# Cached token keys turned in squares by Vector with queries spread by token group, and memory queries' single rows copied first

## The chip, the cores and the metric

The kernel runs on one core of a Trainium2 chip. The time is the device time of one execution in microseconds, from the first instruction to the last; the median of several runs is compared. The engines are PE (matrix products and transposes into PSUM), DVE (Vector), ACT (Scalar), POOL (GpSimd) and SP, which issues most DMAs. Each engine works through its own list of instructions in order and waits where an instruction needs another engine's result.

## The reference

One layer of a decoder, run on a prompt of 512 rows and on 8 samples of 4 new rows each (32 rows), with the same weights. The layer is an mLSTM head group and a differential-attention head group side by side, one output projection, a cross-attention into 256 memory tokens, and a gated feed-forward part with a short convolution. The change touches the two attentions of the samples. The differential attention of a sample has 4 heads with two components of 64 dimensions, 256 cached tokens and its own 4 new ones:

```python
def diff_attend(q, k, v, mask, lam):
    s = jnp.einsum('bqhcd,bkhcd->bhcqk', q.astype(jnp.float32), k.astype(jnp.float32)) * (DA_QK_DIM ** -0.5)
    s = jnp.where(mask[None, None, None], s, -jnp.inf)
    p = jax.nn.softmax(s, axis=-1)
    a = p[:, :, 0] - lam * p[:, :, 1]
    return jnp.einsum('bhqk,bkhd->bqhd', a, v.astype(jnp.float32))
```

For the samples k and v are the cached rows followed by the new ones, and new row t sees all cached tokens and the new ones up to t. The memory attention has 4 heads of 256 dimensions, 256 tokens that differ from sample to sample, and a plain softmax. The mLSTM part also writes out the samples' updated states, C = decay * C + k v^T for 8 samples and 4 heads.

## The kernel before, in words

The program goes through the layer stage by stage: input projection (L485), mLSTM and differential attention with their DMAs, output projection (L411 to L413), memory attention, feed-forward. A scheduler puts the instructions that the code emits into one fixed list for each engine, by its own estimate of when each can start; two helpers bind it: `burst(t)` keeps an instruction right behind t, and `tc.issue_after(t)` keeps it somewhere behind t. `pipe(n, stages...)` emits the stages of n items a step apart, and `F.run` puts filler work between (here the gating of the mLSTM output, L1039 to L1046). Tiles come from pools with a fixed number of buffers: six staging tiles (`stage()`, printed as wst), four weight slots (tag W), three PSUM buffers of tag at, five of tag mm.

**The state update of the samples.** For each of 8 pairs of a sample group and a head, POOL makes vz (L942), PE multiplies it with the keys kS (L1006, tile mlus, a buffer of tag at), and DVE does four updates (L1008), 32 in all. The old and new states lie in staging tiles. The input projection's last part (L485 with hT and wslot) runs on PE at the same time.

**The prompt's differential attention.** For each of 16 pairs of a query block and a head: scores on PE (L1256, L1257, tile sda), maximum on DVE (L1259), exponential on ACT (L1260), normalising on DVE (L1262 to L1264, result pda), transposes on PE (L1272, tile tpa), copy on ACT (L1274), product with the values on PE (L1284, tile oda). The number of keys grows from 128 to 512. PE takes the turn of one pair between the scores of later ones.

**The samples' differential attention, cached keys.** It runs a step at a time beside the prompt's. `dk_load` fetches two pages of 128 tokens by 4 heads by 128 into a staging tile. `dk_turn` makes 8 transposes of 128x128 on PE (L1228) and copies each page's four from PSUM to kT, one page by ACT, one by DVE (L1229); POOL appends the 4 new keys' columns (L1224). `dk_scores` works on two samples at once: 4 products each of 32x260 (L1241), each to its own 32 rows of the result, which hold 4 heads by 2 components by 4 samples by 4 rows, of which one sample's are wanted. DVE adds the mask of the new tokens (L1244), and takes the maximum (L1052); ACT takes the exponential with its sum (L1053). When all 8 are done, `sample_softmax` builds selecting matrices from 1/sum and lambda, and 8 products (L1072) normalise, subtract and put the samples below each other; then two transposes on PE (L1085) and eight copies on ACT (L1089) give daz, from which the products with the values follow (L1340), and for the new tokens L1318, L1320 and L1345.

**The memory attention.** The queries' projection gives 8 groups of 128 columns (`ev_q(m)`). From its PSUM result ACT makes qh (L1429), DVE ql = result - qh (L1430), and ACT qs, the samples' 32 rows (L1432). After every second group `mq_spread` copies qs to the diagonal blocks of qx, by POOL, the last group half by ACT (L1415, L1418). The cached keys of the memory are turned by DVE in place in 32x32 squares (L1502), and the scores are products of them with qx (L1519), for a token group and a head at a time; e picks one half of the heads. The components' sums (L1535), one softmax with maxima and sums over the token groups (L1539 to L1544, L1552 to L1556), and products with an identity that turn the result (L1565) follow. Beside it the prompt's memory scores (L1450, tile sca), exponentials (L1456, tile cp), normalising (L1459), transposes (L1468, tile cpt) go on.

## Time and profile before

| what | value |
|---|---|
| median of 3 runs | 942.89 us (941.97 to 945.42) |
| the profiled execution, its own time | 941.59 us |
| its span in the trace | 939.8 us |
| PE busy | 914.5 us, 97% of the span |
| DVE, ACT, POOL busy | 608.5, 378.2, 221.6 us |
| mean granted clock of PE | 0.994 |
| stretch of the samples' cached keys on PE | 245.4 us (first L1228) to 272.9 (last L1241 starts) |
| first product of the output projection (L411) | 299.95 us |
| first memory score product (L1519) | 432.9 us |

A row of the order of time gives the start in us, the length of the group in us, engine, line, operation, output and inputs, shape, and the number of instructions; in square brackets the idle time before it and what ended it. A product in full precision shows as two records on PE. A busy PE counts overlapping matmuls once. The span starts with the first instruction; the execution's own time is some 1.8 us longer.

### The profile page before, as it was taken

How to read it: one execution, taken by the hardware profiler on the slowest of the kernel's cores; microseconds unless marked ns; L12 is line 12 of the kernel's file. 1: busy time of each engine (PE TensorE's matmuls, PEld its weight loads, DVE VectorE, ACT ScalarE, POOL GpSimd, SP SyncE). 2: the span in 40 equal slices, each digit the busy share in tenths (PEclk: the TensorE clock that was granted, in tenths of full speed). 3: DMA queues.
4: the chain of work that ended last, by engine and by line, in shares of the span. 5: the costliest groups of instructions: out<-in, count | busy, mean ns of one | idle time of the engine just before them, and what ended most of it. 6: DMA issues, size and time to landing. Idle time of an engine off the chain costs nothing. (4 is left out here: it accounts for less than half of the span.)

```text
span 939.8 us, 17453 instructions
## 1 busy us (share of the span) xinstructions
PE 914.5 (97%) x6778; PEld 799.9 (85%) x6778; DVE 608.5 (65%) x1130; ACT 378.2 (40%) x728; POOL 221.6 (24%) x474
## 2 busy tenths in 40 slices
PE   7999999999999999998999999999999999999995
PEld 5899787879866778997877899889988998999974
DVE  5845144565887439586744778637757785676767
ACT  5745233344576447624534533322212222222232
POOL 6611000024442116471000553001100110110114
PEclk9999999999999999999999999999999999999998
DMA  8950023335780439957845642062054204412023
GB/s 274 317 187 8 1 90 138 90 107 157 247 292 7 141 112 314 311 183 238 343 155 159 198 130 72 27 179 69 8 153 121 88 21 109 139 48 90 24 94 117
DMA packets 120834, 130.59 MB, mean 139 GB/s; under 512 B 8599, under 2 KB 86264, under 8 KB 120752
## 3 DMA queue, kind: packets, MB, share of 16 engines
q1 hardware_dynamic: 114568, 125.96, 42.9%
q10 hardware_dynamic: 6184, 3.53, 1.2%
q8 instruction: 53, 0.87, 0.4%
q14 instruction: 29, 0.24, 0.1%
HBM read 112.54 MB, written 16.93 MB: 138 GB/s over the span
## 5 line engine op out<-in xcount | busy, mean ns | idle before, releaser
L485 PE MATMUL mm<-fT,wslot 128*128 128x256 f32 x1872 | 236.0, 288 | 0.0
L485 PEld LDWEIGHTS mm<-fT,wslot 128*128 128x128 f32 x1872 | 234.4, 188 | 1.8 <-issue 0.8
L146 ACT CAST wslot<-wst 128x1024 fp32r<-128x1024 f32 x125 | 130.7, 1049 | 255.5 <-issue 70.8
L147 DVE TENSOR_TENSOR wslot<-wst,wslot 128x1024 fp32r<-128x1024 f32 x125 | 154.7, 1241 | 78.3 <-ACT wslot L146 77.8
L1836 PE MATMUL mm<-wslot,act 128*128 128x512 f32 (+1 forms) x180 | 69.3, 387 | 0.0
L1839 PE MATMUL mm<-wslot,act 128*128 128x512 f32 (+1 forms) x172 | 67.0, 391 | 0.0
L1840 PE MATMUL mm<-wslot,act 128*128 128x512 f32 (+1 forms) x172 | 66.8, 392 | 0.0
L1738 POOL COPY cvo<-u 128x2 f32<-128x2 f32 x43 | 10.4, 242 | 217.2 <-DVE u L1736 217.2
L411 PE MATMUL mm<-wslot,hT 128*128 128x512 f32 x128 | 51.3, 402 | 0.0
L413 PE MATMUL mm<-wslot,hT 128*128 128x512 f32 x128 | 51.0, 400 | 0.0
L485 PE MATMUL mm<-hT,wslot 128*128 128x256 f32 (+1 forms) x384 | 50.9, 289 | 0.0
L412 PE MATMUL mm<-wslot,hT 128*128 128x512 f32 x128 | 50.8, 397 | 0.0
L1733 DVE TENSOR_TENSOR u<-mm,rsb 128x256 f32<-128x256 f32 x43 | 18.1, 423 | 48.8 <-PE mm L485 48.8
L485 PEld LDWEIGHTS mm<-hT,wslot 128*128 128x128 f32 x384 | 49.2, 188 | 0.5 <-issue 0.2
L1836 PEld LDWEIGHTS mm<-wslot,act 128*128 128x128 f32 x180 | 34.3, 191 | 8.0 <-issue 0.8
L1840 PEld LDWEIGHTS mm<-wslot,act 128*128 128x128 f32 x172 | 32.3, 188 | 6.9 <-issue 0.4
L1839 PEld LDWEIGHTS mm<-wslot,act 128*128 128x128 f32 x172 | 32.3, 188 | 6.9
L1750 ACT ACTIVATE c<-c 128x560 f32<-128x560 f32 x21 | 14.1, 672 | 56.8 <-DVE c L1744 56.7
L1744 DVE SCALAR_TENSOR_TENSOR c<-u,cvT,c 128x560 f32<-128x560 f32 x43 | 34.3, 798 | 0.9
L1743 DVE SCALAR_TENSOR_TENSOR c<-u,cvT,c 128x560 f32<-128x560 f32 x43 | 34.1, 793 | 0.2
L1851 DVE TENSOR_TENSOR yp<-mm,yp 128x512 f32<-128x512 f32 (+1 forms) x41 | 27.1, 672 | 4.8 <-PE mm L1840 4.6
L413 PEld LDWEIGHTS mm<-wslot,hT 128*128 128x128 f32 x128 | 24.1, 188 | 5.0
(493 smaller groups left out, 1858.3 us busy)
## 6 DMA issues: line engine op xcount, KB each, us to landing
wst<-in_w_up_dram SPq DMA_DIRECT2D x42, 512.0 KB
wst<-in_w_in_dram SPq DMA_DIRECT2D x28, 512.0 KB
wst<-in_w_down_dram SPq DMA_DIRECT2D x20, 512.0 KB
kvt<-in_cache_mem_k_dram SPq DMA_DIRECT2D x10, 512.0 KB
kvt<-in_cache_mem_v_dram SPq DMA_DIRECT2D x10, 512.0 KB
wst<-in_w_mk_dram SPq DMA_DIRECT2D x8, 512.0 KB
xb<-in_x_prompt_dram SPq DMA_DIRECT2D x8, 512.0 KB
wst<-in_cache_dk_dram SPq DMA_DIRECT2D x16, 256.0 KB
```

The source lines that it names most:

```text
L146: nc.scalar.copy(out=hi, in_=src)
L147: (eng or nc.vector).tensor_tensor(out=lo, in0=src, in1=f32(hi), op=SUB)
L411: mm(ps[b], lhsT=xt.hi(k, c0, c0 + n), rhs=s[:, 0, kk, :], start=(k == 0), stop=False)
L412: mm(ps[b], lhsT=xt.hi(k, c0, c0 + n), rhs=s[:, 1, kk, :], start=False, stop=False)
L413: return mm(ps[b], lhsT=xt.lo(k, c0, c0 + n), rhs=s[:, 0, kk, :], start=False, stop=(k == nk - 1))
L485: mm(ps[i], lhsT=s[:, l, k, :], rhs=x(k, c0, c1), start=(k == 0 and j == 0), stop=(k == 7 and j == 2))
L1743: STT(out=c, in0=u[:, 1:EXT - 1], scalar=w[1], in1=c, op0=MUL, op1=ADD)
L1744: STT(out=c, in0=u[:, 0:EXT - 2], scalar=w[0], in1=c, op0=MUL, op1=ADD)
L1836: mm(ps, lhsT=t[:, 0, c0:c0 + P], rhs=s[:, 0, i % 2, cs], start=st, stop=False)
L1839: mm(ps, lhsT=t[:, 0, c0:c0 + P], rhs=s[:, 1, i % 2, cs], start=False, stop=False)
L1840: return mm(ps, lhsT=t[:, 1, c0:c0 + P], rhs=s[:, 0, i % 2, cs], start=False, stop=en)
L1851: VTT(out=y, in0=ps, in1=y, op=ADD)
```

## The change

Part one. The samples' cached keys are no longer transposed on PE: `dk_turn` is now one DVE instruction that turns the staging tile of 128x1024 in place in squares of 32x32 (L1235). The queries are spread beforehand into qx, a tile in a weight slot, cleared (L1214) and filled by 16 copies (L1217) on POOL, so that each token group of 32 rows meets its own queries; 8 products of 32x128 per sample (L1262), in bursts of their own for each sample, give the scores of all token groups, and ACT copies them to sc (L1265). The staging tile is held until these products. The scores of the new tokens come from `dk_new` (L1241, L1248 to L1251). When all samples are done, `dk_sum` adds the parts with 32 products (L1280), and one softmax for all samples (`da_softmax`, L1087 to L1102) takes maxima and sums over the token groups with two small 32-column transposes each (`over_groups`, L1055 to L1060); `attend` turns the result with 32 products (L1073) and two copies (L1076). The kT tiles, the per-sample mask, maximum and exponential, and L1072, L1085 and L1089 go. `over_groups`, `hcols` and `attend` are now shared with the memory part, whose own text moves up unchanged.

Part two. In `ev_q` the samples' rows qs and the spread are emitted ahead of qh and ql (L1464 to L1469), and `mk_scores` goes over e outside and over the samples inside, with both samples' PSUM tiles open at once (L1542 on).

```diff
+    def over_groups(t, n, u, w, op):
+        nc.vector.transpose(out=u, in_=t)
+        VRED(out=v2(w, TS), in_=u.rearrange("p (n g t) -> p n t g", n=2, g=4), axis=AX.X, op=op)
+        if op == ADD:
+            nc.vector.reciprocal(out=w, in_=w)
+        VCP(out=u.rearrange("p (n g t) -> p n g t", n=2, g=4), in_=v2(w, TS).unsqueeze(2).broadcast_to([P, 2, 4, TS]))
+        nc.vector.transpose(out=t, in_=u)
...
+        for c in range(2):
+            for h in range(H):
+                for g in range(4):
+                    with burst(t):
+                        t = mm(pT[NS * g:NS * g + NS, c * P + NS * h:c * P + NS * h + NS], lhsT=a[:, 64 * h + NS * c:64 * h + NS * c + NS],
+                               rhs=view(ident, 4 * g, [(16, NB), (1, TS)]), start=True, stop=True).ins
...
+    qx = wp.tile([P, 4, NB, H, 4, TS], F32, name="qx", tag="W")
+    nc.gpsimd.memset(qx, 0.0)
+    for g in range(4):
+        for j in range(4):
+            nc.gpsimd.tensor_copy(out=qx[NS * g:NS * g + NS, j, :, :, g, :],
+                                  in_=dqT[NS * j:NS * j + NS, :, SEQ:].rearrange("p h (b t) -> p b h t", t=TS))
...
     def dk_turn(b):
-        kt = kts[b] = wp.tile([P, H, 260], F32, name="kT", tag="W")
-        nc.gpsimd.tensor_copy(out=kt[:, :, 256:260], in_=dkT[:, :, SEQ + TS * b:SEQ + TS * (b + 1)])
-        for g in range(2):
-            ps = at("tpk")
+        nc.vector.transpose(out=kst[b], in_=kst[b])
...
-                tr(ps[:, h * P:(h + 1) * P], kst[b][g][:, h * P:(h + 1) * P], ident)
-            (VCP if g else nc.scalar.copy)(out=kt[:, :, g * P:(g + 1) * P], in_=v2(ps, P))
...
     def dk_scores(b):
-        if b % 2 == 0:
-            return
...
+        for e in range(2):
+            for j in range(4):
+                with burst(t):
+                    t = mm(ps[NS * j:NS * j + NS, e * P:e * P + P].rearrange("p (h c t) -> p h c t", h=2, c=2),
+                           lhsT=qx[:, j, b, 2 * e:2 * e + 2].rearrange("p h g t -> p (h g t)"),
+                           rhs=view(kst[b], 256 * e + NS * j, [(P, 2), (512, 2), (1, NS)]), start=True, stop=True).ins
+        nc.scalar.copy(out=sc[:, b], in_=ps)
...
             if i == 1:
                 nc.scalar.mul(out=qs[:, m, :], in_=ps[:, n:n + NS], mul=1.0 / 16.0)
                 if m % 2 == 1:
                     mq_spread(m // 2)
+            nc.scalar.mul(out=q, in_=ps[:, :n], mul=1.0 / 16.0)
+            STT(out=ql[m // 4][:, m % 4, c0:c0 + n], in0=ps[:, :n], scalar=1.0 / 16.0, in1=f32(q), op0=MUL, op1=SUB)
```

What this does to the order of PE, where the input projection ends. Before (mm is the projection, mlus the state update's products, sda and tpa the prompt's scores and turns, tpk the turns of the samples' keys):

```order
L485 MATMUL mm<-hT_263,wslot 128x288
L1006 MATMUL mlus<-vz,kS 128x512 x2
L1256 MATMUL sda<-dkT,dqT 128x128
L1257 LDWEIGHTS cb
L1257 MATMUL sda<-cb 128x128
L1256 MATMUL sda<-dkT,dqz 128x128
L1257 LDWEIGHTS cb
L1257 MATMUL sda<-cb 128x128
L1256 MATMUL sda<-dkT,dqT 128x128
L1228 MATMUL tpk<-cpk,wst 128x128 x4
L1257 LDWEIGHTS cb
L1257 MATMUL sda<-cb 128x128
```

Six of the eight L1006 stand further ahead, 8 to 11 projection products apart, the first 65 products before the projection's end. After, behind the projection's end (sx is the new tokens' scores, ssc the samples' scores, mlt the gating's transposes):

```order
L1006 MATMUL mlus<-vz,kS 128x512
L1292 MATMUL sda<-dkT,dqz 128x128
L1293 LDWEIGHTS cb
L1293 MATMUL sda<-cb 128x128
L1006 MATMUL mlus<-vz,kS 128x512 x3
L1248 MATMUL sx<-dkT,qw 128x32 x2
L1262 MATMUL ssc<-wst,qx 32x128 x8
L1006 MATMUL mlus<-vz,kS 128x512
L1248 MATMUL sx<-dkT,qw 128x32 x4
L1039 MATMUL mlt<-cpk,mlh 128x128 x4
L1248 MATMUL sx<-dkT,qw 128x32 x2
L1039 MATMUL mlt<-cpk,mlh 128x128 x8
L1308 MATMUL tpa<-cpk,pda 128x128
```

The first two L1006 stand 13 and 5 products before the projection's end and the third behind the first prompt scores; the last four rows of that kind are here, behind the projection and mixed with the first samples' scores. The turns tpk are gone, and the first tpa comes behind the gating's transposes.

DVE, in the same place. Before, from the first state update to the first pda (kT is a copy of the turned keys):

```order
L1008 SCALAR_TENSOR_TENSOR wst<-wst,dec,mlus 128x128 x20
L1022 TENSOR_TENSOR gq<-gq,mlrs 128x1
L1008 SCALAR_TENSOR_TENSOR wst<-wst,dec,mlus 128x128 x4
L1024 TENSOR_SCALAR mlhs<-numS,gq 128x128
L1008 SCALAR_TENSOR_TENSOR wst<-wst,dec,mlus 128x128 x8
L1259 TENSOR_REDUCE nm<-sda 128x1 x4
L1229 COPY kT<-tpk 128x4x128
L1262 RECIPROCAL rc<-su 128x2
L1229 COPY kT<-tpk 128x4x128
L1263 TENSOR_SCALAR rc<-rc,su,nlam 128x1
L1262 RECIPROCAL rc<-su 128x2
L1264 SCALAR_TENSOR_TENSOR pda<-pda,rc 128x128
```

After, from the first state update on:

```order
L1008 SCALAR_TENSOR_TENSOR wst<-wst,dec,mlus 128x128 x8
L1295 TENSOR_REDUCE nm<-sda 128x1
L1008 SCALAR_TENSOR_TENSOR wst<-wst,dec,mlus 128x128 x4
L1295 TENSOR_REDUCE nm<-sda 128x1 x2
L1008 SCALAR_TENSOR_TENSOR wst<-wst,dec,mlus 128x128 x4
L1295 TENSOR_REDUCE nm<-sda 128x1
L1008 SCALAR_TENSOR_TENSOR wst<-wst,dec,mlus 128x128 x8
L1298 RECIPROCAL rc<-su 128x2
L1008 SCALAR_TENSOR_TENSOR wst<-wst,dec,mlus 128x128 x4
L1298 RECIPROCAL rc<-su 128x2
L1235 STREAM_TRANSPOSE wst<-wst 128x1024
L1299 TENSOR_SCALAR rc<-rc,su,nlam 128x1 x2
```

The updates are now mixed with the prompt's maxima and the first of six transposes of the keys (wst) that stand here; two others stand further ahead. The third pda, for which the third tpa waits, stood before at the end of this run of work:

```order
L1259 TENSOR_REDUCE nm<-sda 128x1 x2
L1244 TENSOR_TENSOR ssc<-ssc,cpk 128x4 x2
L1052 TENSOR_REDUCE snm<-ssc 128x1 x2
L1045 TENSOR_TENSOR mltm<-mlt,soT 128x512
L1262 RECIPROCAL rc<-su 128x2
L1045 TENSOR_TENSOR mltm<-mlt,soT 128x512 x2
L1263 TENSOR_SCALAR rc<-rc,su,nlam 128x1
L1259 TENSOR_REDUCE nm<-sda 128x1 x2
L1045 TENSOR_TENSOR mltm<-mlt,soT 128x128
L1264 SCALAR_TENSOR_TENSOR pda<-pda,rc 128x128
```

And after:

```order
L1045 TENSOR_TENSOR mltm<-mlt,soT 128x128
L1235 STREAM_TRANSPOSE wst<-wst 128x1024
L1295 TENSOR_REDUCE nm<-sda 128x1 x2
L1298 RECIPROCAL rc<-su 128x2
L296 COPY xts<-mltm 128x128
L1235 STREAM_TRANSPOSE wst<-wst 128x1024
L1299 TENSOR_SCALAR rc<-rc,su,nlam 128x1
L1298 RECIPROCAL rc<-su 128x2
L1300 SCALAR_TENSOR_TENSOR pda<-pda,rc 128x128
```

All eight transposes of the keys are now ahead of the third pda; before, its row followed the copies, masks and maxima of the first samples.

ACT, in the memory attention where the last two groups of queries are taken. Before:

```order
L1456 ACTIVATE cp,csu<-sca,cnm 128x256 x2
L1429 ACTIVATE qh<-mm 128x256 x2
L146 CAST pT<-cpt 128x256
L1432 ACTIVATE qs<-mm 128x32
L1415 COPY qx<-qs 32x2x8x4 x8
```

And after:

```order
L1491 ACTIVATE cp,csu<-sca,cnm 128x256 x2
L1468 ACTIVATE qh<-mm 128x256
L1465 ACTIVATE qs<-mm 128x32
L1468 ACTIVATE qh<-mm 128x256
L146 CAST pT<-cpt 128x256
L1450 COPY qx<-qs 32x2x8x4 x8
```

The samples' rows qs now stand ahead of the last qh, and the spread (x8) behind the same cast of pT as before. PE at the first scores of the memory's keys, before:

```order
L1450 MATMUL sca<-mkT,qh 128x256 x2
L1450 MATMUL sca<-mkT,ql 128x256
L1519 MATMUL ssc<-wst,qx 32x2x32 x64
L1468 MATMUL cpt<-cpk,cp 128x128 x4
L1450 MATMUL sca<-mkT,qh 128x256 x2
```

And after:

```order
L1485 MATMUL sca<-mkT,ql 128x256
L1554 MATMUL ssc<-wst,qx 32x2x32 x34
L1503 MATMUL cpt<-cpk,cp 128x128 x4
L1554 MATMUL ssc<-wst,qx 32x2x32 x30
L1485 MATMUL sca<-mkT,qh 128x256 x2
```

The 64 products are now in two pieces with the four transposes of cp between them; the first 32 of them are those of the first half of the heads for both samples.

More of the change, by code (lines that the diff above doesn't have):

```diff
@@ new lines, in dk_scores, with dk_sum @@
+        nc.scalar.copy(out=sc[:, b], in_=ps)
+        last[0] = t
+    last = [None]
+    def dk_sum():
+        t = None
+        for i in range(NB // 2):
+            for c in range(2):
+                r = slice(64 * c, 64 * c + 64)
+                for h in range(2):
+                    for e in range(2):
+                        o = 48 * h + 16 * (1 - e)
+                        with tc.issue_after(last[0]) if t is None else burst(t):
+                            t = mm(hcols(pS[c][NS * i:NS * i + NS], h), lhsT=con("selE")[r, o:o + NS],
+                                   rhs=hcols(sc[r, 2 * i + e], h), start=(e == 0), stop=(e == 1)).ins
@@ L1290, in da_end @@
             da_post(outs[i // H], P, i // H * P)
[L1292 to L1293 removed]
     W.nslots = 0
     prompt = pipe(4 * H, da_soft, lambda i: None, da_turn, da_av, da_end)
[L1298 to L1299 removed]
+    sc = S([P, NB, 256], F32, "sc")
+    gs = T2([P, 136], "gs")
+    nc.gpsimd.memset(gs, 1.0)
+    xn = gs[:, 128:136]
     for t, _ in enumerate(pipe(NB, dk_load, dk_turn, dk_scores)):
```

170 lines of the change are left out of this document (70 added, 100 removed).

## Prediction

> **What bounds the kernel now.** I read the page first, then the waits of the PE, then busy time by stretch, then the order of time in two places.
>
> ```profile
> PE 914.5 (97%) x6778; PEld 799.9 (85%) x6778; DVE 608.5 (65%) x1130; ACT 378.2 (40%) x728; POOL 221.6 (24%) x474
> ```
>
> The waits of PE (engine, tile and line, releaser: us in total, times, longest):
>
> ```profile
> PE ssc L1519 <- POOL qx L1415: 3.7, 1, 3.7
> ...
> PE tpa L1272 <- DVE pda L1264: 1.4, 2, 1.1
> ...
> PE spt L1565 <- DVE spc L1556: 0.8, 1, 0.8
> ```
>
> PE is busy 914.5 of 939.8 us. Its longest wait of all is 3.7 us in the memory scores (L1519), for the spread queries; part two of the change is aimed at it. Part one works in the stretch of the differential attention, so the stretch matters more than the share over the span:
>
> ```profile
> 220.00:230.80 10.80, 10.80 (x151) 9.66 (x149) 5.00 (x13) 8.07 (x18) 5.60 (x11) 1.00 0.23 75
> 252.00:260.00 8.00, 7.69 (x77) 5.99 (x67) 8.00 (x25) 7.63 (x27) 5.93 (x8) 1.00 0.99 351
> 300.00:432.80 132.80, 132.50 (x859) 116.38 (x857) 82.88 (x112) 65.59 (x126) 57.11 (x116) 1.00 0.64 205
> ```
>
> Columns: stretch, length, then busy PE, PEld, DVE, ACT, POOL, granted clock, DMA share, GB/s. From 252 to 260, amid the prompt's first query blocks and the samples' keys, DVE is busy 8.00 of 8.00 us, more than PE. It is 65% over the span, but here it has nothing to give. From 300 on PE is busy 132.50 of 132.80 us, so a delay at 300 goes to the end whole, and so does a gain.
>
> **Part one: the cached keys.** What PE does there, in order of time (the row at 455.38 is the memory part's own sum over components, which part one copies):
>
> ```profile
> 241.50 2.78 PE L485 MATMUL mm<-hT,wslot 128*128 128x288 f32 x21
> 244.12 0.62 PE L1006 MATMUL mlus<-vz,kS 128*128 128x512 f32 x2
> ...
> 246.29 1.55 PE L1228 MATMUL tpk<-cpk,wst 128*128 128x128 f32 x12
> ...
> 250.49 0.33 PE L1272 MATMUL tpa<-cpk,pda 128*128 128x128 f32 x1
> 251.37 1.08 PE L1241 MATMUL ssc<-kT,qz 128*32 128x260 f32 x16
> ...
> 257.01 0.33 PE L1272 MATMUL tpa<-cpk,pda 128*128 128x128 f32 x1 [0.31 <-DVE pda L1264]
> 277.80 1.09 PE L1072 MATMUL spa<-das,csz 128*32 128x260 f32 x16
> 286.08 1.96 PE L1340 MATMUL ops<-vt,daz 128*32 128x128 f32 x64
> 299.95 0.48 PE L411 MATMUL mm<-wslot,mixT 128*128 128x512 f32 x1
> 455.38 1.97 PE L1535 MATMUL pS<-sc,cpk 128*32 128x128 f32 x26
> ```
>
> And DVE:
>
> ```profile
> 235.05 3.57 DVE L1008 SCALAR_TENSOR_TENSOR wst<-wst,dec,mlus 128x128 f32<-128x128 f32 x12 [0.19 <-PE mlus L1006]
> 244.55 2.16 DVE L1008 SCALAR_TENSOR_TENSOR wst<-wst,dec,mlus 128x128 f32<-128x128 f32 x8 [1.53 <-PE mlus L1006]
> 246.62 0.88 DVE L1259 TENSOR_REDUCE nm<-sda 128x1 f32<-128x128 f32 x4
> 247.42 0.68 DVE L1229 COPY kT<-tpk 128x512 f32<-128x512 f32 x1
> 250.10 0.33 DVE L1264 SCALAR_TENSOR_TENSOR pda<-pda,rc 128x128 f32<-128x128 f32 x1
> 250.35 0.27 DVE L1263 TENSOR_SCALAR rc<-rc,su,nlam 128x1 f32<-128x1 f32 x1
> 253.94 1.27 DVE L1045 TENSOR_TENSOR mltm<-mlt,soT 128x512 f32<-128x512 f32 x2
> ```
>
> The memory part turns its cached keys on DVE already, 128x1024 at a time (ns: shortest, median, longest):
>
> ```profile
> L1502 DVE STREAM_TRANSPOSE kvt<-kvt x10: 1201/1245/1246, 416.3 to 438.1; 128x1024 f32<-128x1024 f32 x10
> ```
>
> PE's own work about breaks even. Removed: 64 transposes at 1.55/12 = 0.13 us, 8.3; four score bursts of 1.08, 4.3; L1072, 1.1; two transposes, 0.25: 14.0 us. Added: eight bursts of 16 records at 1.96/64 = 0.031 each plus some 0.2 of start and end, 5.5 in all; 64 records of the sums (L1280), whose nearest row is L1535 at 1.97/26 = 0.076, so 4.5 (between 2.0, if they overlap like L1340, and 4.9); 64 records of L1073, 2.0 at most by the same 0.031, I take 1.6; sixteen of the new keys (L1248), 0.5: 12.1 us. By this alone the part gains 1.9 us.
>
> DVE is where it costs. A sample's transpose becomes one DVE pass of 1.245 us; what DVE did for it before was one copy of 0.68. The Trainium skill ("VectorE: DVE Perf Modes", The three transpose paths) lists 311 ns for a 128x128 bf16 transpose on Vector against 390 ns on TensorE; by that table the exchange favours Vector, while these rows give 1.245/8 = 0.156 us for 128x128 on DVE against 0.13 on PE.
>
> More weighs the order, as the change section shows. Before, six of the eight L1006 products stand inside the projection's matmuls and DVE does 24 of its 32 state updates (L1008) by 243; only 8 are left at 244.55. After, two of the eight products stand near the end of that projection and six behind it. Four L1006 leave the projection, at 0.31 each or less (0.62 for two), so it ends near 243; the first product is 13 matmuls ahead of that, 13 x 2.78/21 = 1.7 us. DVE begins its updates at about 241.4. From there its order is one in-order stretch, and the third turn of the prompt's probabilities on PE (tpa) waits for the pda at its end:
>
> - 32 updates at 3.57/12 = 0.298 (0.27 in the other row): 9.2 us
> - six transposes at 1.245: 7.5
> - four gate products of 512 at 0.64 and one of 128: 2.9
> - eight maxima at 0.22: 1.8
> - three pda at 0.33, 1.0, and ten of L1298 and L1299, 0.27 at most; I take 0.14, as each starts before the one ahead has ended (250.35 behind 250.10 + 0.33): 2.4
> - the new keys' four (L1249 to L1251) and three small ones, between 0.14 and 0.45, the size of pda; I take 0.3: 2.1
>
> That is 25.9 us, with some 0.5 for waits: the third tpa at 267.8 instead of 257.01. The lag is 10.8 us. PE cannot use it: its order has the transposes no more that filled it, and it is in order. Up to the first pda the same sum gives 254 instead of 250.49, so PE idles some 2.5 us before the first tpa and some 4 before the third, the rest in small holes between.
>
> Two other engines were looked at. POOL now clears and fills qx ahead of vz, which L1006 needs. A clearing of 64x2048 beside it is one row:
>
> ```profile
> 220.13 1.80 POOL L1208 MEMSET dqz<- 64x2048 f32 x1
> ```
>
> So the clearing is about 1.8 us and sixteen copies of 32x128, at the 2.16/8 = 0.27 of L1415 below, are 4.3: 6.1 us. The row 220.00:230.80 above shows POOL's work until it turns to vz, and that POOL is free for the rest of those 10.8 us; what it has free takes nearly all of the 6.1, so I cost it at nothing. Without that cover it is up to 3 us, all of it in DVE's stretch. The keys' buffers are held until the scores instead of the turns, so the last samples' loads issue later, on a DMA that is 0.99 full at 252 to 260; a late one would stand in the same stretch on DVE, with pda behind it. I count nothing for it and leave it in the upper bound.
>
> From the third tpa to the first L411, before takes 299.95 - 257.01 = 42.9 us. Of that the change takes away 28 transposes (3.6), three score bursts (3.3), L1072 (1.1) and the two transposes (0.25), and adds five bursts (3.4), the sums (4.5) and L1073 (1.6): 44.2. The one softmax is a chain of some 22 short DVE instructions between the sums and L1073; four rounds of prompt work lie over it. If that cover is thin, PE waits there as at L1565 (0.8 us); I take 0.5. So L411 comes at about 267.8 + 44.2 + 0.5 = 312.5: **part one costs 12.5 us**. Bounds: 6, if the transposes find gaps and DVE's short instructions overlap more than summed; 18, if the idle halves the clock and the softmax stalls.
>
> What idle does to the clock, in this trace, is seen in part two:
>
> ```profile
> 438.50:440.60 2.10, 2.10 (x82) 2.00 (x70) 1.84 (x5) 1.04 (x5) 0.00 (x0) 0.50 0.46 75
> ```
>
> ```profile
> 432.86 0.65 PE L1519 MATMUL ssc<-wst,qx 128*32 128x64 f32 x32
> 437.19 3.56 PE L1519 MATMUL ssc<-wst,qx 128*32 128x64 f32 x96 [3.67 <-POOL qx L1415]
> 442.94 1.10 PE L1519 MATMUL ssc<-wst,qx 128*32 128x64 f32 x64
> ```
>
> ```profile
> 431.33 0.66 ACT L1429 ACTIVATE qh<-mm 128x256 fp32r<-128x256 f32 x2
> 434.24 0.57 DVE L1459 TENSOR_SCALAR cp<-cp,csu 128x256 f32<-128x256 f32 x2
> 435.50 0.20 ACT L1432 ACTIVATE qs<-mm 128x32 f32<-128x32 f32 x1 [3.26 <-DVE ql L1430]
> 435.76 2.16 POOL L1415 COPY qx<-qs 32x64 f32<-32x64 f32 x8 [10.94 <-ACT qs L1432]
> ```
>
> After 3.67 us of idle the granted clock is 0.50 from 438.5 to 440.6, and 96 products take 3.56 us, against 96 x 1.10/64 = 1.65 at full clock: the halving cost 1.9 us. One such after the wait of 4 us in part one would cost as much at most; I leave it out of the sum, since PE works in pieces between its waits there, and give it to a rival below. The Trainium skill ("TensorE: Matmul & The Clock Gate", What's actually happening) says that an idle window of about 3.4 us halves the clock and that about as long of work restores it; by that rule one halving would cost about 1.7 us (an estimate), and the row at 0.50 agrees with it.
>
> **Part two: the memory queries.** Before, the last copy of single rows (L1432) stands on ACT behind both qh, and it waits 3.26 us for DVE's ql: both read the same result. DVE comes to ql late, behind L1459. After, qs stands ahead of the last qh; ACT reads the result at 431.33, so qs is done by 431.8, the spread's 8 copies on POOL and the 8 on ACT by 434 to 434.5 instead of 437.9. With the loop turned, PE first does the 32 products that need no last spread, then two more, then four transposes of cp (ready at 434.24 + 0.57 = 434.8), then the rest. So PE waits from 433.5 to 434.8: 1.3 us instead of 3.67. Saved: 2.4 of wait and 3.56 - 1.65 = 1.9 of clock: **4.3 us**. Bounds: 2.4, if the clock drops all the same; 6, if cp is early, since the keys' loads come ahead of a PE that is later. What comes late next is cp, and behind it DVE's transposes, not the queries. Moving qs costs ACT nothing new; POOL had idled 10.94 us.
>
> **Sum.** +12.5 - 4.3 = +8.2 us on the profiled execution's own 941.59 us (span 939.8): 949.8. That execution lies 1.3 us under the median of the runs, 942.89 (0.14%); on the median it would be 951.1. I say 950.
>
> **The rivals.** A change of 0.5% (4.7 us) is about what a measurement of this kernel can tell from none: below 938.2 faster, above 947.6 slower.
>
> - *PE's balance decides* (faster). If DVE's stretch runs ahead of PE, because its updates start earlier than I read or because PE's tpa is not really held by the transposes ahead of it, then part one gives its 1.9 us and part two 4.3: 942.9 - 6.2 = 937. For it: PE is 97% busy and the copies of 0.6 to 0.68 us for eight samples go. Against it: DVE at 8.00 of 8.00 from 252 to 260, and PE already waited for pda there (1.4 us). It decides if the lag at the third tpa is under 3 us. Chance 0.15.
> - *The lag is half.* DVE recovers about 5 us because some updates or transposes land in the holes before 241 or behind the third tpa: part one +5 to 6, part two -4.3: 944. Chance 0.2.
> - *The clock halves too.* The waits of 2.5 and 4 us lie 10 us apart; if one or both are followed by 0.50, at 1.9 each as in part two, another 2 to 4 us; with a stall of 2 to 3 at the softmax, 954 to 957. For it: the 3.67 us of idle above had that effect. Against it: no wait of PE in 244 to 300 is that long now. Chance 0.2.
> - *The change doesn't reach the wait at L1519*: cp or the keys' transposes hold PE as long as the queries did. Then part two gives 0 to 1: 954. Chance 0.05, counted to the slower side.
>
> **How the numbers follow.** My forecast, 947 to 953, has 0.4; with the two slower rivals, 0.65 for slower. Same: 0.2. Faster: 0.15. The range leaves out most of the first rival and the worst of the third: 940 to 957. The slower cases' own range is 947.6 to 957.
>
> **What would show it.** Right: DVE's first L1008 near 241; the third tpa near 268; PE idle 6 to 9 us between 250 and 270, released by DVE's pda; the first L411 near 312; the longest wait at the memory scores under 2 us and their clock near 1. Wrong: the first L411 at 302 or earlier, DVE with holes in 244 to 268, or PE's main wait there at the sums or L1073, which would mean that the softmax chain and not the transposes sets the time.

## The result and the profile after

The changed kernel takes 957.66 us (median of 6 runs, 955.08 to 959.50) against 942.55 before (6 runs, 941.82 to 945.42): a ratio of 1.0153 [1.0139, 1.0167] (the quotient of the two medians is 1.0160), 15.1 us slower where 8 were forecast, and just above the end of the range, 957. The profiled execution took 958.23 us with a span of 956.5, 16.6 us more than the one before. All medians and ratios here are of executions that lie within 1% of each other; only the version with all three remedies also had two far slower ones, 1292.51 and 1824.81 us, which are left out of its median.

| mark | before | after | later by |
|---|---|---|---|
| third tpa (prompt's third turn of probabilities) | 257.01 | 268.81 | 11.8 |
| first L411 (output projection) | 299.95 | 316.12 | 16.2 |
| first memory score | 432.86 | 450.62 | 17.8 |
| first sum over components of the memory part | 455.38 | 469.37 | 14.0 |
| end of the span | 939.8 | 956.5 | 16.7 |

So most of the loss arises before 316, part two gives 3.8 back, and the rest adds 4.3. The waits of PE after, in the same columns as before:

```profile
PE tpa L1308 <- DVE pda L1300: 5.4, 2, 4.8
PE spt L1073 <- DVE spc L1101: 2.4, 1, 2.4
PE mlt L1039 <- DVE gq L1022: 2.0, 1, 2.0
PE ssc L1554 <- DVE ql L1469: 1.7, 1, 1.7
```

PE now waits mostly for DVE, and at the memory scores 1.7 us instead of 3.7. By stretch (length, busy PE, PEld, DVE, ACT, POOL, granted clock, DMA share, GB/s):

```profile
244.00:253.00 9.00, 6.04 (x57) 4.29 (x57) 9.00 (x36) 3.82 (x12) 2.22 (x6) 1.00 0.86 262
253.00:273.00 20.00, 12.40 (x85) 8.39 (x83) 13.62 (x32) 7.45 (x25) 5.45 (x5) 0.51 0.86 292
...
263.30:268.80 5.50, 0.68 (x2) 0.40 (x3) 4.07 (x10) 2.15 (x8) 1.67 (x2) 0.50 0.89 309
268.80:273.00 4.20, 4.19 (x26) 2.81 (x27) 1.80 (x7) 1.77 (x6) 0.00 (x0) 0.50 1.05 402
...
316.10:450.60 134.50, 132.79 (x859) 116.59 (x857) 81.57 (x113) 66.19 (x130) 58.68 (x122) 1.00 0.62 203
```

Two readings. Up to 253 DVE has no hole and PE a third of the time idle: the DVE-bound stretch that was forecast. From 253 to 273 both are partly idle: PE 12.40 of 20 us, DVE only 13.62. Something other than DVE's own work ends waits there, and the clock stands at 0.51. DVE in order of time shows what:

```profile
241.61 2.35 DVE L1008 SCALAR_TENSOR_TENSOR wst<-wst,dec,mlus 128x128 f32<-128x128 f32 x8 [9.20 <-PE mlus L1006]
...
254.16 1.25 DVE L1235 STREAM_TRANSPOSE wst<-wst 128x1024 f32<-128x1024 f32 x1 [1.01 <-issue]
...
257.90 1.24 DVE L1235 STREAM_TRANSPOSE wst<-wst 128x1024 f32<-128x1024 f32 x1 [0.73 <-DMA wst<-in_cache_dk_dram]
...
263.49 1.25 DVE L1235 STREAM_TRANSPOSE wst<-wst 128x1024 f32<-128x1024 f32 x1 [0.99 <-DMA wst<-in_cache_dk_dram]
...
266.88 1.25 DVE L1235 STREAM_TRANSPOSE wst<-wst 128x1024 f32<-128x1024 f32 x1 [1.25 <-DMA wst<-in_cache_dk_dram]
...
268.32 0.35 DVE L1300 SCALAR_TENSOR_TENSOR pda<-pda,rc 128x128 f32<-128x128 f32 x1
```

The turns of 128x1024 wait for loads of the cached keys, three times in this stretch, and the pda behind the last of them is the one for which the third tpa waits. SP's issues show why the loads are late. Before, the last load of keys was issued by 253.3 (249.50 + 3.79):

```profile
249.50 3.79 SPq L1094 DMA_DIRECT2D wst<-in_cache_dk_dram  x6
```

After, four are issued at 259.88, and the state updates' stores (L1010) stand between the loads:

```profile
247.33 1.95 SPq L1010 DMA_DIRECT2D out_dram<-wst  x3
250.58 0.92 SPq L1107 DMA_DIRECT2D wst<-in_cache_dk_dram  x2
...
252.22 1.94 SPq L1107 DMA_DIRECT2D wst<-in_cache_dk_dram  x4
...
259.88 1.88 SPq L1107 DMA_DIRECT2D wst<-in_cache_dk_dram  x4
```

From 235 to 275 SP's queue waits 6.6 us for those stores to end before it may load into their staging tiles, against 3.5 before (first row); the longest such wait, 4.9 us, stands ahead of the last four loads:

```profile
SPq L1094 <- DMA out_dram<-wst: 3.5, 3, 2.5
SPq L1107 <- DMA out_dram<-wst: 6.6, 4, 4.9
```

The prediction had named the scores as what holds these loads; in this trace none of their waits is for the scores.

PE, in order of time:

```profile
253.17 0.30 PE L1308 MATMUL tpa<-cpk,pda 128*128 128x128 f32 x1
...
268.81 0.45 PE L1308 MATMUL tpa<-cpk,pda 128*128 128x128 f32 x1 [4.83 <-DVE pda L1300]
...
283.09 4.33 PE L1280 MATMUL pS<-sc,cpk 64*32 64x128 f32 x64
...
301.58 0.73 PE L1073 MATMUL spt<-cpk,spc 128*32 128x32 f32 x62 [2.36 <-DVE spc L1101]
...
316.12 0.48 PE L411 MATMUL mm<-wslot,mixT 128*128 128x512 f32 x1
```

And at the memory scores, their first sum and the values product (L1597, the probabilities with the memory's values):

```profile
450.62 0.65 PE L1554 MATMUL ssc<-wst,qx 128*32 128x64 f32 x32
453.02 0.75 PE L1554 MATMUL ssc<-wst,qx 128*32 128x64 f32 x36 [1.74 <-DVE ql L1469]
...
469.37 1.97 PE L1568 MATMUL pS<-sc,cpk 128*32 128x128 f32 x24
...
485.31 4.48 PE L1597 MATMUL pso<-wst,caz 128*32 128x256 f32 x48 [0.96 <-ACT caz L1076]
```

### The profile page after: what moved, and what is told of

Same layout as the page of the kernel before. It is cut to its first block, busy times and chain, and to the rows that moved or that the text cites. A ratio compares the mean times of both kernels' runs of the same rounds, so it can differ in the third digit from the quotient of the medians.

```text
span 956.5 us, 17696 instructions
## 1 busy us (share of the span) xinstructions
PE 920.3 (96%) x6905; PEld 802.5 (84%) x6905; DVE 608.1 (64%) x1135; ACT 373.3 (39%) x707; POOL 227.3 (24%) x484
## 4 chain that ended last, share of the span: by engine, by line
PE 78%; DVE 8%; DMA 7%; ACT 3%; issue 3%; POOL 1%; SPq 1%; DVEq 0%; ACTq 0%; POOLq 0%
PE mm L485 30%; PE mm L412 6%; PE mm L413 6%; PE mm L411 6%; PE mm L472 4%; PE mm L1847 4%; PE mm L1851 3%; PE mm L1850 3%; DMA wst<-in_cache_mem_k_dram 1%; PE mm L390 1%; PE sda L1292 1%; DVE wslot L147 1%; PE cpo L1515 1%; DVE xb L1178 1%; PE pso L1597 1%
## 5 line engine op out<-in xcount | busy, mean ns | idle before, releaser
L485 PE MATMUL mm<-fT,wslot 128*128 128x256 f32 x1872 | 236.0, 288 | 0.0
L485 PEld LDWEIGHTS mm<-fT,wslot 128*128 128x128 f32 x1872 | 234.4, 188 | 1.8 <-issue 0.8
L411 PE MATMUL mm<-wslot,hT 128*128 128x512 f32 x128 | 51.3, 402 | 0.0
L485 PE MATMUL mm<-hT,wslot 128*128 128x256 f32 (+1 forms) x384 | 50.3, 289 | 0.0
L485 PEld LDWEIGHTS mm<-hT,wslot 128*128 128x128 f32 x384 | 48.6, 188 | 0.4 <-issue 0.2
L1862 DVE TENSOR_TENSOR yp<-mm,yp 128x512 f32<-128x512 f32 (+1 forms) x41 | 27.1, 672 | 5.1 <-PE mm L1851 5.1
```

Source lines behind the costliest of these rows:

```text
L411: mm(ps[b], lhsT=xt.hi(k, c0, c0 + n), rhs=s[:, 0, kk, :], start=(k == 0), stop=False)
L485: mm(ps[i], lhsT=s[:, l, k, :], rhs=x(k, c0, c1), start=(k == 0 and j == 0), stop=(k == 7 and j == 2))
```

## The experiments

Ratios are to the kernel before on the same chip (its median there 941.8 to 942.3 us). None leaves out a part of the computation. A difference in us between two versions is one of their medians, partly across chips; the medians of the kernel before differ by up to 0.7 us (941.8 to 942.6).

### Which part costs

**Part two alone**, on the kernel before:

```diff
-            nc.scalar.mul(out=q, in_=ps[:, :n], mul=1.0 / 16.0)
-            STT(out=ql[m // 4][:, m % 4, c0:c0 + n], ...
             if i == 1:
                 nc.scalar.mul(out=qs[:, m, :], in_=ps[:, n:n + NS], mul=1.0 / 16.0)
                 if m % 2 == 1:
                     mq_spread(m // 2)
+            nc.scalar.mul(out=q, in_=ps[:, :n], mul=1.0 / 16.0)
+            STT(out=ql[m // 4][:, m % 4, c0:c0 + n], in0=ps[:, :n], scalar=1.0 / 16.0, in1=f32(q), op0=MUL, op1=SUB)
...
+        ps = {b: mmp("ssc")[:, :256] for b in bs}
+        for e in range(2):
+            for b in bs:
```

> The kernel before with part two alone. If the wait for the spread queries was the whole cost there (theory), the wait of 3.7 us shrinks to about 1.7 as in the changed kernel, the clock stays at 1.00, and the time is 3.7 us (3 to 4.5) under before: 939. If what the scores gain is given back at the products with the memory's values, as the halved clock there in the changed kernel's trace suggests (rival), 941 to 942.5.

Measured: 938.84 us, 0.9965 [0.9951, 0.9979]. Part two is a gain of 3.0 us by itself.

**Part one alone**: both edits put back in the changed kernel.

```diff
+            nc.scalar.mul(out=q, in_=ps[:, :n], mul=1.0 / 16.0)
+            STT(out=ql[m // 4][:, m % 4, c0:c0 + n], ...
             if i == 1:
...
-            nc.scalar.mul(out=q, in_=ps[:, :n], mul=1.0 / 16.0)
-            STT(out=ql[m // 4][:, m % 4, c0:c0 + n], ...
...
-        ps = {b: mmp("ssc")[:, :256] for b in bs}
-        for e in range(2):
-            for b in bs:
+        for b in bs:
+            ps = mmp("ssc")[:, :256]
+            for e in range(2):
```

> The changed kernel with part two undone. If the two parts add up (theory), it is 3 to 4.5 us above the changed kernel: 961 to 962. If part two's gain is lost behind part one anyway (rival), it is the changed kernel's time, 957.7.

Measured: 960.31, 1.0180 [1.0152, 1.0208]; L411 starts at 317.15 and PE waits 3.6 us for the spread queries again. The whole loss, some 18 us, is part one's, more than the 12.5 forecast.

**The copy's place alone**: only the lines of `ev_q` moved in the kernel before, the loops of the scores as they were.

```diff
-            nc.scalar.mul(out=q, in_=ps[:, :n], mul=1.0 / 16.0)
-            STT(out=ql[m // 4][:, m % 4, c0:c0 + n], ...
             if i == 1:
...
+            nc.scalar.mul(out=q, in_=ps[:, :n], mul=1.0 / 16.0)
+            STT(out=ql[m // 4][:, m % 4, c0:c0 + n], ...
```

> The kernel before with only the first half of part two: the single rows copied and spread ahead of qh and ql, the loop over samples and heads as it was. If the copy's place is what counts (theory), the scores wait 1 to 2 us instead of 3.7 and the time is that of part two alone, 938 to 939.5. If the turned loop is what hides the last spread, the wait stays at 2.5 us or more: 940 to 941.5.

Measured: 938.41, 0.9957 [0.9944, 0.9970]. Its scores:

```profile
433.42 0.65 PE L1519 MATMUL ssc<-wst,qx 128*32 128x64 f32 x32
434.50 2.29 PE L1519 MATMUL ssc<-wst,qx 128*32 128x64 f32 x96 [0.43 <-POOL qx L1415]
```

Moving one copy on ACT ends the wait of 3.67 us; 0.43 is left. The 96 products behind it take 2.29 us at a granted clock of 1.00, against 3.56 at half clock before, so by these rows the halving there cost 1.3 us, where the prediction took 1.9. The turned loop adds nothing that can be measured.

### What in the order costs

**The fill of qx behind the last vz on POOL**, so that the L1006 products get their old places:

```diff
-        GTT(out=vzs[i], ...
+        vlast[0] = GTT(out=vzs[i], ...
...
+    with tc.issue_after(vlast[0].ins):
         nc.gpsimd.memset(qx, 0.0)
```

> The changed kernel with the clearing and filling of qx on POOL put behind the last vz, which sends the products L1006 back to their old places inside the projection. Theory one (the state updates, late and in one stretch with the turns on Vector, hold the third tpa): third tpa near 260 instead of 268.8, first L411 near 306, 947 to 949 in all. Rival (the loads of the cached keys end the turns' waits, whatever Vector does before): third tpa at 265 or later, 954 or more. Second rival (PE's own added work and the softmax chain): no more than 2 us better than the changed kernel, 956.

Measured: 953.86, 1.0123 [1.0106, 1.0140]. The third tpa comes at 261.91, nearly 7 us sooner, but the delay returns at the next turn:

```profile
261.91 0.33 PE L1308 MATMUL tpa<-cpk,pda 128*128 128x128 f32 x1 [0.51 <-ACT pda L1296]
...
268.32 0.33 PE L1308 MATMUL tpa<-cpk,pda 128*128 128x128 f32 x1 [3.43 <-DVE pda L1300]
...
314.44 0.48 PE L411 MATMUL mm<-wslot,mixT 128*128 128x512 f32 x1
```

The late updates are real, but only 1.7 us of the 16 at L411 go away with them: the pda stands behind turns that wait for loads, whatever is ahead of them. Here SP's last loads of keys are held 5.0 us by the scores (L1262) and issued by 260.4, hardly sooner than the 261.8 of the changed kernel. At L1073 the gain is still 3.4 us (298.22 against 301.58); half of it is lost again behind, where the granted clock is 0.50 from 300.2 to 302.2 and was 1.00 in the changed kernel.

**The turn of sample b behind the prompt's pda b** on DVE, so that a turn waiting for its load holds no probability up:

```diff
+        with tc.issue_after(pdas[b]):
+            nc.vector.transpose(out=kst[b], in_=kst[b])
...
+        pdas[i] = STT(out=pt[:, 0, :nk], ...).ins
```

> The changed kernel with the turn of sample b's keys on Vector put behind the prompt's pda of pair b; the state updates stay late. Theory one (the turns stand ahead of the third pda): three turns fewer ahead of it, third tpa at 262 to 263, the products with the scores then wait 2 to 3 us for turns instead: 950 to 953 in all. Rival (the loads): the third tpa comes early, but the scores wait for turns that wait for loads, 955 to 957.

Measured: 953.77, 1.0131 [1.0108, 1.0154]. PE's wait changes its name:

```profile
PE ssc L1262 <- issue: 6.8, 4, 3.6
```

The pda is on time, but now PE's scores of the samples stand ahead of the tpa and come late; the third tpa is at 264.17, L411 at 314.29. "issue" here is a wait that the profile does not assign; that it is for the turns follows from the times, as each of the four ends 0.09 or 0.10 us after a turn has ended (the longest at 262.56, behind a turn from 261.23 that takes 1.23).

**The keys of samples 6 and 7 in a weight slot**, free earlier than the staging tiles:

```diff
-        kst[b] = stage()
+        kst[8] = wp.tile([P, 2, 1024], F32, name="ks", tag="W") if b == 6 else kst.get(8)
+        kst[b] = kst[8][:, b - 6] if b > 5 else stage()
```

> The changed kernel with the keys of samples 6 and 7 loaded into a weight slot, so that their loads needn't wait until the scores of samples 0 and 1 give two staging tiles back. If turns that wait for loads are part of what holds the third pda (theory two), Vector's last two waits for loads (0.99 and 1.25 us) go, the third tpa comes near 266.5 instead of 268.8, and the time is 2 to 2.5 us under the changed kernel: 955.4. If only Vector's own work counts (theory one alone), or the loads are bound by what the DMA can carry, it stays within 0.7 us: 957 to 958.

Measured: 953.18, 1.0126 [1.0095, 1.0156]; the wait before the third tpa falls from 4.83 to 2.38 us and L411 comes 3.3 us sooner:

```profile
265.56 0.45 PE L1308 MATMUL tpa<-cpk,pda 128*128 128x128 f32 x1 [2.38 <-DVE pda L1300]
...
312.83 0.48 PE L411 MATMUL mm<-wslot,mixT 128*128 128x512 f32 x1
```

About 1.0 us of these 3.3 was there ahead of any turn (the first L1006 stands at 240.21 instead of 241.18); the shorter wait is as large as the rest. So the loads' lateness is a cost of its own, besides DVE's work.

In these three traces L411 comes 1.7, 1.8 and 3.3 us sooner, but the span is 4.9, 5.2 and 7.0 us shorter. The difference lies behind L411, in code that none of the edits touches: from there to the end the changed kernel's trace needs 640.4 us, these three 637.2, 637.0 and 636.7. The values product, at half clock in the changed kernel's trace alone of the four, is 1.7 of it. So a good part of what the medians give back is not the remedies' own.

**Fill late, and the slot**:

```diff
+    with tc.issue_after(vlast[0].ins):
...
+        kst[b] = kst[8][:, b - 6] if b > 5 else stage()
```

> The same on top of the late filling of qx (953.9). Theory two: the state updates are early, and the turns of samples 6 and 7 no longer wait; third tpa near 260, 950 to 951.5. Theory one alone: as with the late filling, 953 to 954.5. If the turns of samples 2 to 5, which wait for staging tiles that the states' stores give back, hold the stretch anyway: 952.5 to 954.

Measured: 954.43, 1.0133 [1.0102, 1.0163]: a miss. With a tile for them free earlier, the scheduler put the turns of samples 6 and 7 at 259.64 and 262.02, ahead of the prompt's next pda at 266.19, and each waited for its load all the same:

```profile
259.64 1.25 DVE L1235 STREAM_TRANSPOSE ks<-ks 128x1024 f32<-128x1024 f32 x1 [1.59 <-DMA ks<-in_cache_dk_dram]
262.02 1.25 DVE L1235 STREAM_TRANSPOSE ks<-ks 128x1024 f32<-128x1024 f32 x1 [0.76 <-DMA ks<-in_cache_dk_dram]
266.19 1.05 DVE L1300 SCALAR_TENSOR_TENSOR pda<-pda,rc 128x128 f32<-128x128 f32 x1
```

The two remedies do not add up unless the turns are held behind the pda as well.

**All three together**:

```diff
+    with tc.issue_after(vlast[0].ins):
...
+        kst[b] = kst[8][:, b - 6] if b > 5 else stage()
...
+        with tc.issue_after(pdas[b]):
```

> All three: filling of qx late, each turn behind the prompt's pda of its pair, keys of samples 6 and 7 in a weight slot. Theory two: neither pda nor scores wait for loads beyond 2 us in all; first L411 near 307, 947 to 949. If the scores wait for turns as they did with the turns behind pda alone (6.8 us): 951 to 954. If the change's own work on PE and the one softmax are most of the cost: 951 or more with no wait for turns.

Measured: 947.94 (median of four executions), 1.0074 [1.0045, 1.0104]. Of this kernel only the timed runs are used, so where its waits lie is not shown. By the ratio half of the loss is gone, where each remedy alone returned about 4 us by the medians and 2 to 3 by the ratios.

**And the scores one step later**, so that PE meets them when they are turned:

```diff
-    for t, _ in enumerate(pipe(NB, dk_load, dk_turn, dk_scores)):
+    for t, _ in enumerate(pipe(NB, dk_load, dk_turn, lambda b: None, dk_scores)):
```

> The last kernel with the scores one step later in the pipeline, so that PE meets turned keys. Theory two: the scores' wait for turns goes to under 1 us, 1 to 3 us better than without the step, 945 to 948. If the softmax chain, which starts a step later, sets the end: no better, or up to 2 us worse, with a longer wait at L1073.

Measured: 944.47, 1.0021 [1.0003, 1.0039]. The turns on PE are back near their places, and L411 is 8.0 us sooner than in the changed kernel:

```profile
258.19 0.27 PE L1308 MATMUL tpa<-cpk,pda 128*128 128x128 f32 x1
...
294.34 0.76 PE L1073 MATMUL spt<-cpk,spc 128*32 128x32 f32 x64 [0.48 <-DVE spc L1101]
...
308.13 0.48 PE L411 MATMUL mm<-wslot,mixT 128*128 128x512 f32 x1
```

```profile
253.00:273.00 20.00, 16.65 (x163) 11.86 (x162) 18.78 (x43) 13.22 (x44) 7.68 (x8) 0.89 0.89 320
```

DVE is busy 18.78 of 20 us again and PE 16.65. The new order and one more tile for the keys are together worth 13.2 us by the medians. In the traces it is 14.0 us, of which 8.0 lie ahead of L411 and 6.0 behind it, where nothing was edited. SP's queue still waits 6.9 us for the stores (4.4 the longest), but each turn now stands behind the pda of its pair. Part two is in this kernel too, so part one, well ordered, still costs about 5 to 6 us (2.3 over before, with 3.0 to 3.9 given back by part two).

### The clock and the sums

**Twenty unread products in PE's wait ahead of the third tpa**, to keep the clock up (the computation is whole; nobody reads them):

```diff
+        for k in range(20 if i == 1 else 0):
+            with burst(summed[0].ins):
+                mm(op[:, 256:512], lhsT=identb, rhs=warm[:, 0:256], start=True, stop=True)
```

> The changed kernel with 20 bf16 products of 128x256 that nobody reads, put on PE into the wait of 4.8 us ahead of the third tpa; they write unused columns of a PSUM tile. If the halved clock behind that wait costs time (the rival of the prediction), PE comes back to full clock by the third tpa, the work from there to 273 takes 2.3 us instead of 4.4, and the time is 1.5 to 2.5 us under the changed kernel: 955 to 956. If Vector's stretch alone sets the pace and the clock costs nothing, 957.7 as before, within 0.7; if the products overrun the wait, 958 to 959.

Measured: 955.64, 1.0148 [1.0133, 1.0163]. The clock behind the wait is full:

```profile
268.80:273.00 4.20, 4.20 (x53) 3.09 (x51) 2.54 (x10) 3.73 (x16) 0.00 (x0) 1.00 1.06 399
```

PE starts 53 records there instead of 26, and from the third tpa (267.01) to the first sum (279.04) it takes 12.0 us instead of 14.3. But the time is not separable from the changed kernel's 1.0153 [1.0139, 1.0167]. The softmax wait is the same 2.36 us:

```profile
297.52 0.73 PE L1073 MATMUL spt<-cpk,spc 128*32 128x32 f32 x62 [2.36 <-DVE spc L1101]
...
313.74 0.47 PE L411 MATMUL mm<-wslot,mixT 128*128 128x512 f32 x1
```

Behind it the granted clock is 0.50 from 299.5 to 301.5 in this trace and 1.00 in the changed kernel's, and from L1073 to L411 PE takes 16.2 us instead of 14.5. So the halved clock behind the third tpa did cost about 2.3 us, and 1.7 of them were lost again at another wait. From 253 to 263.5, ahead of the filler, the clock is 0.50 here too; what that costs was not tried.

**The sums in another order**, so that neighbouring products go to different 32-row groups:

```diff
-        for i in range(NB // 2):
-            for c in range(2):
-                r = slice(64 * c, 64 * c + 64)
-                for h in range(2):
-                    for e in range(2):
+        for c in range(2):
+            r = slice(64 * c, 64 * c + 64)
+            for h in range(2):
+                for e in range(2):
+                    for i in range(NB // 2):
```

> The changed kernel with the sums over components (L1280) in another order: neighbours go to different 32 rows of the result instead of the same. If the 4.3 us of these 64 records come from neighbours that wait for each other on the same rows (theory), they take about 2 us and the time falls by 1.5 to 2.3 us: 955.4 to 956.2. If each product costs 0.068 us whatever its neighbour, no change: 957 to 958.

Measured: 954.26, 1.0119 [1.0100, 1.0138], 3.4 us less than the changed kernel.

```profile
283.84 0.63 PE L1280 MATMUL pS<-sc,cpk 64*32 64x128 f32 x14
285.97 1.33 PE L1280 MATMUL pS<-sc,cpk 64*32 64x128 f32 x50
```

The same 64 records take 1.96 us instead of 4.33, and the wait of 2.36 us at L1073 is gone, as the softmax starts sooner after the third tpa (269.60 here, yet L411 is at 313.63, 44.0 us behind it instead of 47.3). The sums and the wait together fell by 4.7 us; 3.3 of them arrive, as a tpa at 293.26 now waits 1.73 us for its pda, where it waited 0.54.

**The same rotation in the memory part's sums**, with part two alone:

```diff
-        for i in range(NB // 2):
-            for h in range(2):
-                for e in range(2):
+        for h in range(2):
+            for e in range(2):
+                for i in range(NB // 2):
```

> The kernel before with part two and with the memory's sums over components in the other order as well. If neighbours on the same rows cost 0.076 instead of 0.031 us each, the 32 records of these sums take 1.3 us less, and the time is 937.5 to 938.5. If the softmax behind them starts later, since the sums come apart in PE's order: 938.8 as with part two alone, or more.

Measured: 938.38, 0.9958 [0.9942, 0.9973], no better than part two alone. The sums shrink (0.40 + 0.43 + 0.84 us for the 32 records), and the next wait takes the gain:

```profile
465.38 0.76 PE L1566 MATMUL spt<-cpk,spc 128*32 128x32 f32 x64 [2.09 <-DVE spc L1557]
```

In part two alone that wait was 0.82 us. Here DVE's softmax decides; in the samples' attention PE's lateness did too. The versions with part two alone are the fastest; no version with part one beats the kernel before.

## Why the prediction was right in direction and short in size

Of its 8.2 us against 16.6 in the profiled execution, term by term:

| term | forecast | measured | difference |
|---|---|---|---|
| third tpa later | +10.8 | +11.8 | 1.0 |
| third tpa to L411, against 42.9 before | 44.7 | 47.3 | 2.6 |
| L411 to the memory scores | 0 | +1.6 | 1.6 |
| part two, to the first sum | -4.3 | -3.8 | 0.5 |
| behind the sums | 0 | +2.7 | 2.7 |

**The late start and the in-order stretch: right.** DVE's first L1008 came at 241.61 (241.4), the first tpa at 253.17 (254), the third at 268.81 (267.8), and PE stood idle for pda before it. But of PE's idle time from 250 to 270, some 9.6 us, only 4.8 is for pda; 2.0 is for gq, 1.6 for mltm (both DVE) and 1.2 for ACT's new copy of the scores (L1265).

**What fills the stretch: two errors that cancelled.** The forecast had 25.9 us of DVE work and 0.5 of waits. From 241.61 to the end of the pda at 268.67 are 27.1 us, of which DVE waits 1.01 + 0.73 + 0.99 + 1.25 = 4.0, so its work is 23.1: 2.8 too much was counted for the work, and the waits were 3.5 too small. That the third tpa came out within 1.0 us was therefore luck, and the prediction's own sign of being wrong, "DVE with holes in 244 to 268", did appear. The step that failed reads "I count nothing for it and leave it in the upper bound", on the late loads. The states' stores hold the staging tiles (in the version with the late fill the scores do), and so the waits for the loads stand in the stretch on DVE. Runs: with the keys of two samples elsewhere the wait at the third tpa falls by 2.4 us; with the L1006 back in place the delay stays at the next turn. No edit alone returns more than 4.5 us by the medians, and no more than 3.3 at L411, since each takes one of several waits that end near the same time; three of them return 9.7 (7.4 by the ratios), and a step's distance to the scores 3.5 more (5.0).

**From the third tpa to L411: the softmax wait was mis-sized.** It was given 0.5 us and took 2.36. The statement that four rounds of prompt work lie over it was wrong in amount: the chain on DVE, interleaved with that work, takes 14.5 us from its first instruction (286.99, as the sums end) to the last that L1073 needs.

```profile
286.99 0.89 DVE L1087 TENSOR_REDUCE gs<-pS 128x4 f32<-128x256 f32 x2 [1.46 <-PE pS L1280]
...
301.10 0.43 DVE L1101 TENSOR_TENSOR spc<-spc 128x256 f32<-128x256 f32 x1
```

The sums themselves were right: 4.33 us against 4.5. L1073 took 0.8 us (301.58 to 302.34) against 1.6. That leaves about 1.8 of the 2.6. The clock, which was 0.50 to 273, covers it: the run with filler, at full clock from 268.8 on, needs 2.3 us less to the first sum. The clock was a rival with 954 to 957 for its time and a chance of 0.2. The halving came, 0.50 lasted from 254 to 273, and the rival's other half, a stall of 2 to 3 us at the softmax, came true as well; of all the forecasts it came closest to 957.66.

**Part two: right, the waiting object not.** 3.8 us here and 3.0 to 3.9 alone, against 4.3. The wait fell by 1.9 us (2.4 were forecast), and the 192 score products take 3.77 us instead of 5.31, 1.5 less (1.9 were forecast for the clock). The forecast held cp for what is late next (1.3 us). The trace has 1.74 for DVE's ql. That ql still reads a PSUM tile which the second open score tile takes is argued, not tried; the version without the turned loop, which waits 0.43 for qx, fits it. The clock stayed at full speed at the scores, as forecast.

**Behind it: not foreseen.** Of the 8.4 us by which the profiled time was missed, 4.3 lie behind L411, where the forecast had nothing. From L411 to the scores PE has 1.7 us of waits instead of 0.3: 0.8 in a projection (L485) for DVE's ql, 0.6 in a product with the prompt's values (L1320) for ACT's aT, and the 0.3 of before. Of the 2.7 us behind the sums 1.7 is the values product, 48 records in 4.48 us instead of 2.80 in the trace before, at a clock of 0.66 in that stretch:

```profile
485.00:490.00 5.00, 4.69 (x51) 2.89 (x52) 0.33 (x1) 0.21 (x2) 0.00 (x0) 0.66 0.92 336
```

The traces with the late fill, with the turns behind pda and with the slot have the same code there and need 3.2 to 3.7 us less from L411 to the end, so most of this loss is not a fixed price of the change.

**The rivals.** PE's balance and the half lag fell: PE did wait at pda. That the change might not reach the wait at L1519 fell too.

**What stays open**: the rest of part one's cost in its best order, 5 to 6 us, was not taken apart further; the sums in rotated order were not tried in it. Its third tpa is only 1.2 us later than before and its L411 8.2 us, so what is left lies between the two, where the scores now stand that were moved back, and the sums with 4.32 us. Of these 8.2 its trace gains 1.7 back between L411 and the memory scores (131.2 us against 132.9), for a reason not traced. The clock's chance behind short waits, told below, is in every comparison of single traces here.

## What to carry to other kernels

When an engine takes over work from PE, follow its whole in-order list to the result that PE waits for, the loads that this work waits for included: a load whose tile is freed by a store or a score is a wait on that engine, with everything behind it. One remedy alone shows little where several such waits end close together; judge the order with all of them mended. Before giving a remedy its gain, see where in the trace the gain lies; here much of it lay behind the stretch that was edited. And before a longer change is costed, try its cheap part by itself: one copy moved ahead of two lines gave all of part two's gain.

## What the runs showed of the hardware

**Products with 32 columns of weights ran faster when neighbours went to different row groups of the result.** 64 records onto one group after another took 4.33 us, 0.068 each; in rotated order 1.96, 0.031 each, the same as L1340 has in the kernel before. The Trainium skill ("TensorEngine Tiling (Array Packing)", Key Properties) says that tiles operate independently and can load weights and multiply in parallel; the trace agrees for neighbours on different tiles, and shows that neighbours on one tile don't gain. Half of the old neighbours also added to the same result; the run does not tell this apart from the same group.

**The same waits were followed by half the clock in some traces and not in others.** The values product has 48 records behind waits of 0.84 and 0.96 us in the changed kernel. The runs of part one alone and of part two alone:

```profile
486.33 0.76 PE L1073 MATMUL spt<-cpk,spc 128*32 128x32 f32 x64 [0.84 <-DVE spc L1579]
488.05 4.48 PE L1596 MATMUL pso<-wst,caz 128*32 128x256 f32 x48 [0.96 <-ACT caz L1076]
```

```profile
466.67 0.76 PE L1566 MATMUL spt<-cpk,spc 128*32 128x32 f32 x64 [0.82 <-DVE spc L1557]
468.39 2.80 PE L1587 MATMUL pso<-wst,caz 128*32 128x256 f32 x48 [0.96 <-ACT caz L1569]
```

It is 4.48 us in the changed kernel, with part one alone and with the rotated sums, and 2.80 in the others whose traces are used (behind 2.09 and 0.63 us with the memory's sums rotated). The Trainium skill ("TensorE: Matmul & The Clock Gate", What's actually happening) says that the window in which activity is judged runs freely, and that the point at which the clock changes depends on where in it the first product lands; that would fit, but no run here shows the window. The softmax wait at L1073 does the same. It is 2.35 or 2.36 us in six traces; behind it the clock stays at 1.00 in two (the changed kernel and the one with the slot), and PE reaches L411 14.5 us later. In the other four (part one alone, late fill, late fill with the slot, filler) it falls to 0.50, and L411 is 16.0 to 16.2 us behind.

**Idle in pieces went with half the clock for 20 us.** From 253 to 273 PE was busy 12.40 of 20 us and the granted clock was 0.51. It was 1.00 up to 253 and 0.50 from 254 on, behind a wait of 2.0 us, and stayed there through waits of 1.6, 1.2 and 4.83 us. The share of busy time does not decide it: with the turns behind the pda PE was busy 12.46 of the same 20 us, and the clock was 0.91; in the best order it was busy 16.65 us at 0.89.
